# A two-layer hybrid decoder trunk in split fp32: eight PSUM buffers dealt out as four and four, and the output projection taken by halves of its contraction

## The chip, the cores and the metric

The kernel runs on one core of one Trainium2 chip. The metric is the time of one execution on the device, in microseconds (us). Engines: PE is TensorE (matmuls; PEld is its weight load), DVE is VectorE, ACT is ScalarE, POOL is GpSimd, SP issues the DMAs. PSUM, into which PE writes, has eight banks; each tile of this kernel takes one bank.

## The reference, cut to what matters

Two layers act on a sequence of 256 tokens with 1024 channels. Every layer normalises its input and multiplies it with one wide input weight. From the product three branches are made: retention, a dilated window attention, and a gated depthwise convolution with a layer norm. Each is multiplied by a SiLU gate and projected back to 1024 channels; sigmoid gates merge the three; the output projection closes the layer.

```python
h = rms_norm(x, norm_w)
z = h @ w_in + b_in
rq, rk, rv, rg, aq, ak, av, ag, cu, cg, mg = jnp.split(z, split_points, axis=-1)
...
y_ret = (r * jax.nn.silu(rg)) @ ret_w_o
...
y_att = (a * jax.nn.silu(ag)) @ att_w_o
...
c = jax.nn.silu(layer_norm(c, conv_norm_w, conv_norm_b))
y_conv = (c * jax.nn.silu(cg)) @ conv_w_o
gates = jax.nn.sigmoid(mg).reshape(B, S, N_BRANCHES, D)
merged = gates[:, :, 0] * y_ret + gates[:, :, 1] * y_att + gates[:, :, 2] * y_conv
return x + merged @ w_out
```

After the second layer a last RMS norm makes the output.

## The kernel before

The weights are cut into units of 1024 rows by 256 columns, which `order()` lists; the main loop takes one unit per step. A unit is named by its kind and number: `ya`, `yc` are the projections of attention and convolution (four units each), `mc` the merge gates of the convolution, `wo` the output projection, `cs` and `cl` the two halves of the convolution's input, with which the next layer begins.

Each float32 operand is split into a high and a low part of a type that PE takes faster, and a product is the sum of three matmuls (high by high, high by low, low by high). In step n `load(n + 3)` issues the DMAs of a weight unit into two half tiles `raw`, and `split(n + 2)` makes `whi` on ACT (line 218) and `wlo` on DVE (line 219), a half tile at a time. `raw`, `whi` and `wlo` have five half tiles each. So the second half of unit n + 2 goes where the first half of unit n was, and has to wait until PE has read that for the last time. `split` stands in the program ahead of the matmuls of step n, so on ACT and DVE everything that step n issues afterwards is queued behind it.

There are four ways through a unit. `gemm` and `gemm_values` take the eight slices of k in order, 48 matmuls of 256 columns, and are done with the first half tile at half of the step. `gemm_wide` takes two neighbouring units as a couple, 512 columns at once: a step covers four of the eight slices of k, first for tokens 0 to 127 (t = 0), then for tokens 128 to 255 (t = 1), 24 matmuls, so the first half tile is read again in the second half, until 18 of 24. `gemm_two` does likewise for the first two `wo` units, with 48 matmuls; the other two `wo` units go through `gemm`.

The order on all engines is that of the program. Work is put aside with `later` and played at four places of a step: `after_split`, `inside` (in the middle of the matmuls), `first` (after the matmuls) and `due` (after the unit's own evacuation). What the change touches:

- PSUM tiles come from rings named by tag: `g` (products, 3 buffers), `S` (2), `pt` (2), `u` (1). A new tile of a ring waits until the oldest has been read.
- `branch` (lines 686 and 687) multiplies a finished half of a `yc` couple by its gate and adds it to `m`. `merged` turns four 128 by 128 blocks of `m` on PE (line 699, tile `mt`) and makes from them the operand `mh` of the output projection, its high part on ACT (line 702) and its low part on DVE (line 703).
- `ln_add`, `ln_mean`, `ln_rows` make the mean of the layer norm: DVE adds the channels (`ca`), PE sums over partitions (`ss`, line 330), DVE makes the mean and two diagonal matrices `dg` (line 351), and PE spreads them over the partitions (`rb`, line 357).
- `project` adds a `wo` unit to `x` (line 708); its inner function `rest` squares it (`sq`, line 365) and makes two slices of the next layer's operand `gx`, high part on ACT (line 377), low part on DVE (line 378). The first three `cs` and `cl` steps of the next layer read `gx`, slice after slice.
- `project_last` does it for the last layer, with the transposes `nat` (`turn_out`, line 727) and the sums of squares that end the kernel.

Of the kernel before, what the change touches and what calls it, by code (L numbers as in the profile page):

```python
# [142 lines left out]
def trunk(ctx: ExitStack, tc, xp, wp, b_in, params, consts, out):  # L143
# [42 lines left out]
    def load(n, parts=((0, 4), (4, 8))):  # L186
        if n >= N:
            return
        raw_t[n] = ts = [sb.tile([128, 4, W], F32, tag="raw", name="raw", bufs=5) for _ in range(2)]
        if n in couple:  # L190
            n0 = couple[n]
            src = wp[n0:n0 + 2].rearrange("u p (k n) -> p k u n", n=W)
            for q in range(2):
                k = 4 * (n - n0) + 2 * q
# [26 lines left out]

    def gemm(n, a):

        hs, ls = hi_t.pop(n), lo_t.pop(n)
        k_first = n + 1 < N
        if k_first:
            t = ps.tile([128, 2, W], F32, tag="g", name="g", bufs=3)
            p = halves(t)
        else:
            t = p = [ps.tile([128, W], F32, tag="g", name=f"g{j}", bufs=3) for j in range(2)]  # L230

        def part(j, k):
            wh, wl = hs[k // 4][:, k % 4, :], ls[k // 4][:, k % 4, :]
            t = slice(j * 128, j * 128 + 128)
            trio = ((wh[:, t], a[:, k, 0, :]), (wh[:, t], a[:, k, 1, :]), (wl[:, t], a[:, k, 0, :]))
            for i, (u, v) in enumerate(trio):
                PE.matmul(p[j], u, v, start=(k == 0 and i == 0 and (j == 0 or not k_first)),  # L237
                          stop=(k == NK - 1 and i == 2 and (j == 1 or not k_first)))

        if k_first:  # L240
            for k in range(NK):
                if k == 4:
                    play(inside, n)
                for j in range(2):
                    part(j, k)
        else:
            for j in range(2):
                if j == 1:
                    play(inside, n)
                for k in range(NK):  # L250
                    part(j, k)
        return t

    def gemm_values(n, a):

        hs, ls = hi_t.pop(n), lo_t.pop(n)
        t = ps.tile([128, 2, W], F32, tag="g", name="g", bufs=3)
        for k in range(NK):
            if k == 4:
                play(inside, n)  # L260
            wh, wl = hs[k // 4][:, k % 4, :], ls[k // 4][:, k % 4, :]
            for j in range(2):
                r = slice(j * 128, j * 128 + 128)
                for i, (u, v) in enumerate(((0, wh), (0, wl), (1, wh))):
                    PE.matmul(t[:, j], a[:, k, u, r], v, start=(k == 0 and i == 0 and j == 0),  # L265
                              stop=(k == NK - 1 and i == 2 and j == 1))
        return t

    def gemm_wide(n, a, between):

        hs, ls = hi_t.pop(n), lo_t.pop(n)
        half = n - couple[n]
        if half == 0:
            st["wide"] = [ps.tile([128, 2, W], F32, tag="g", name="g", bufs=3) for _ in range(2)]
        for t, p in enumerate(st["wide"]):
# [10 lines left out]
        return st["wide"][1]  # L286

    def gemm_two(n, a):

        hs, ls = hi_t.pop(n), lo_t.pop(n)  # L290
        half = n - couple[n]
        if half == 0:
            st["two"] = [ps.tile([128, 2, W], F32, tag="g", name="g", bufs=3) for _ in range(2)]
        for u, p in enumerate(st["two"]):
            if u == 1:
                play(inside, n)
            for c in range(4):
                k, d = 4 * half + c, 2 * (c % 2) + u
                wh, wl = hs[c // 2][:, d, :], ls[c // 2][:, d, :]
                for j in range(2):  # L300
                    t = slice(j * 128, j * 128 + 128)
                    trio = ((wh[:, t], a[:, k, 0, :]), (wh[:, t], a[:, k, 1, :]), (wl[:, t], a[:, k, 0, :]))
                    for i, (w, v) in enumerate(trio):
                        PE.matmul(p[:, j], w, v, start=(k == 0 and i == 0 and j == 0),  # L304
                                  stop=(k == NK - 1 and i == 2 and j == 1))
        return st["two"]
# [16 lines left out]
    def token_sums(tiles, ss=None, more=False):  # L323

        start = ss is None
        if start:
            ss = ps.tile([128, 2], F32, tag="S", name="ss")
# [26 lines left out]
    def spread(dg):  # L354
        p = ps.tile([128, S], F32, tag="u", name="rb", bufs=1)
# [173 lines left out]
    def ret_scores(l, h):  # L529
        q, k = st.pop((l, "q", h)), st.pop((l, "k", h))  # L530
        s = ps.tile([128, 384], F32, tag="S", name="rs")
# [10 lines left out]
    def ret_out(l, h):  # L542
        sm, v = st.pop((l, "rsm", h)), st[l, "rv", h - h % 2][:, :, h % 2]
        r = ps.tile([128, 2, W], F32, tag="u", name="r", bufs=1)
# [12 lines left out]
    def ret_back(l, h):  # L557
# [4 lines left out]
        p = ps.tile([128, 2, S], F32, tag="pt", name="rt")  # L562
# [19 lines left out]
    def att_scores(l, pair, g):  # L582
# [6 lines left out]
        for j in range(2):  # L589
            s = ps.tile([128, 2, 128 if g else 256], F32, tag="S", name="as")  # L590
# [29 lines left out]
    def att_turn(l, pair, j, part):  # L620
# [3 lines left out]
        p = ps.tile([128, 2, S], F32, tag="pt", name="pt")  # L624
# [8 lines left out]
    def att_pv(l, pair, j):  # L633
        pts = [st.pop((l, "pts", j, part)) for part in range(2)]
        u = ps.tile([128, S], F32, tag="u", name="u", bufs=1)
# [41 lines left out]
    def branch(l, i, b, n, t, p):  # L677
# [10 lines left out]
        if b == 2:  # L688
            if t == 0:
                later(n, merged, l, i, t, at=first)  # L690
            else:
                later(n + 1, merged, l, i, t, at=inside)

    def merged(l, i, t):

        m, mh = st[l, "m"], st[l, "mh"]
        p = ps.tile([128, 4, 128], F32, tag="pt", name="mt")
# [7 lines left out]
    def project(l, i, n, p):  # L705
# [8 lines left out]
        if i < 3:  # L714
# [5 lines left out]
    def turn_out(k):  # L720
        if k == 0:
            st["nat"] = {}
        for t in range(2):
            half = k // 4
            if k % 4 == 0:
                st["nat"][t, half] = ps.tile([128, 512], F32, name="nat", **NAT[t, half])
            PE.transpose(st["nat"][t, half][:, (k % 4) * 128:(k % 4) * 128 + 128],
                         st["xf"][:, k, t * 128:t * 128 + 128], ident)

    NAT = {(0, 0): dict(tag="pt"), (1, 0): dict(tag="pt"), (0, 1): dict(tag="S"), (1, 1): dict(tag="u", bufs=1)}  # L730
# [4 lines left out]
    def project_last(l, i, n, p):  # L735
        if i == 0:
            st["xf"] = sb.tile([128, NK, S], F32, tag="cacc", name="xf", bufs=1)
        sqs = []
        for j in range(2):
            k = 2 * i + j  # L740
            DVE.tensor_tensor(x[:, k], p[j], x[:, k], ALU.add)
            if i < 3:
                later(n + 1, turn_out, k, at=inside if i == 2 else due)
            else:
                sq = sb.tile([128, S], F32, tag="pts1", name="sq")
                ACT.activation(sq, x[:, k], AF.Square)
                sqs.append(sq)
            DVE.tensor_scalar(st["xf"][:, k], x[:, k], prm[:, P_FINAL + k:P_FINAL + k + 1], None, ALU.mult)
        if i < 3:
            add_squares((l + 1, "sq"), x[:, 2 * i:2 * i + 2], i == 0, i == 2)  # L750
            if i == 2:
                later(n + 1, early_sums, l + 1, at=inside)
            return
        r = rstd(token_sums(sqs, st["ss"]), NORM_EPS)
        turn_out(6)
        turn_out(7)
        for half in range(2):
            for t in range(2):
                o = sb.tile([128, 512], F32, tag="gt", name="o", bufs=4)
                if t == 0:  # L760
                    ACT.mul(o, st["nat"][t, half], r[:, t:t + 1])
                else:
                    DVE.tensor_scalar(o, st["nat"][t, half], r[:, t:t + 1], None, ALU.mult)
# [3 lines left out]
    def finish(n, p):  # L767
        l, kind, i = units[couple.get(n, n)]
# [12 lines left out]
        else:  # L781
            for q, pq in enumerate(p if n in couple else [p]):
                if l + 1 < DEPTH:
                    project(l, i + q, n, pq)
                else:
                    project_last(l, i + q, n, pq if n + 1 == N else halves(pq))

    def finish_wide(n, t, p):
        l, kind, i = units[couple[n]]
        if kind in ("rv", "av"):  # L790
            wide_values(l, kind, i, t, p)
        elif kind in ("mr", "ma", "mc"):
            merge_gate(l, i, kind, t, p)
        else:
            branch(l, i, ("r", "a", "c").index(kind[1]), n, t, p)
# [8 lines left out]
    for l in range(DEPTH):  # L804
# [23 lines left out]
        later(y + 2, ln_mean, l)  # L828
# [23 lines left out]
    def warm_up():  # L852
# [3 lines left out]
        p = ps.tile([128, S], F32, tag="u", name="warm", bufs=1)  # L856
# [7 lines left out]
    with tc.manual_schedule():  # L864
# [24 lines left out]
        for n, (l, kind, i) in enumerate(units):  # L889
# [24 lines left out]
            if kind == "wo" and n in couple:  # L914
                p = gemm_two(n, src)
            elif n in couple:
                p = gemm_wide(n, src, lambda t, p: finish_wide(n, t, p))
# [10 lines left out]
            if n in couple and kind != "wo":  # L928
                if n > couple[n]:
                    finish_wide(n, 1, p)  # L930
            elif n not in couple or n > couple[n]:
                finish(n, p)
            play(due, n)
# [51 lines left out]
```

## Time and profile before

| what | value |
|---|---|
| median of three runs | 1234.7 us (1229.91 to 1234.83) |
| the profiled execution: time / span | 1232.1 us / 1230.3 us |
| PE, PEld busy | 1202.2 us (98%), 1117.9 us (91%) |
| DVE, ACT busy | 976.9 us (79%), 750.3 us (61%) |
| PE's waits for other engines, all | 21.7 us |
| mean granted clock of PE | 0.994 |
| DMA | 214.61 MB, 174 GB/s |

The span runs from the first to the last instruction; 1.8 us of the execution lie around it. Matmuls overlap, so a busy share of 98% isn't an engine at its peak: how long a stretch of matmuls takes is read from their starts.

### The profile page before, as it was taken

The numbers are of one execution on the slowest core, as the hardware profiler recorded it, in microseconds if no ns is written. First come the engines' busy times: TensorE is split into PE (matmuls) and PEld (weight loads), VectorE is DVE, ScalarE is ACT, GpSimd is POOL, SyncE is SP. The second block draws the span as 40 slices with busy tenths as digits, with TensorE's granted clock in tenths as the row PEclk, the third lists the DMA queues.
The fourth block names the chain that finished last, engine by engine and source line by source line (L and its number), as shares of the span: only waits on it lengthen the run. The fifth ranks groups of instructions, "written<-read, shape, count | busy, mean of one in ns | idle before, by whom it ended". The sixth has DMA issues, their size and how long they took to land.

```text
span 1230.3 us, 21469 instructions
## 1 busy us (share of the span) xinstructions
PE 1202.2 (98%) x8260; PEld 1117.9 (91%) x8260; DVE 976.9 (79%) x1705; ACT 750.3 (61%) x1116; POOL 9.2 (1%) x17
## 2 busy tenths in 40 slices
PE   9999999999999999999899999999999999999987
PEld 8999989999999989787899989799999999987977
DVE  6978798888888877775689788989787878768654
ACT  6535467877677666464455446586868686754732
POOL 0000000000000000000000000000000000000000
PEclk9999999999999999999999999999999999999999
DMA  8754566555545565555445554655554545565640
GB/s 310 232 181 145 156 209 196 160 178 166 165 158 179 159 196 182 173 194 169 158 153 186 166 189 140 219 172 181 168 176 146 184 153 169 180 197 179 193 126 35
DMA packets 126711, 214.61 MB, mean 174 GB/s; under 512 B 9744, under 2 KB 95504, under 8 KB 126480
## 3 DMA queue, kind: packets, MB, share of 16 engines
q1 hardware_dynamic: 126608, 213.24, 54.4%
q8 instruction: 65, 1.06, 0.3%
q14 instruction: 38, 0.31, 0.1%
HBM read 212.15 MB, written 1.05 MB: 173 GB/s over the span
## 4 chain that ended last, share of the span: by engine, by line
PE 80%; issue 8%; DVE 6%; DMA 2%; ACT 2%; SPq 0%; POOL 0%; DVEq 0%; POOLq 0%; ACTq 0%
PE g L237 45%; PE g L285 23%; PE g L265 4%; DVE wlo L219 3%; PE as L594 2%; DMA raw<-in_wp 2%; PE u L646 1%; PE pt L628 1%; ACT whi L218 1%; PE g L304 1%; DVE cacc L437 1%; PE rs L533 1%; PE u L641 1%; DMA bb<-in_b_in 0%; ACT Sm L609 0%
## 5 line engine op out<-in xcount | busy, mean ns | idle before, releaser
L219 DVE TENSOR_TENSOR wlo<-raw,whi 128x1024 fp32r<-128x1024 f32 (+1 forms) x387 | 456.0, 1212 | 113.0 <-ACT whi L218 108.5
L218 ACT CAST whi<-raw 128x1024 fp32r<-128x1024 f32 (+1 forms) x387 | 391.7, 1043 | 200.1 <-PE g L285 112.6
L237 PE MATMUL g<-h,whi 128*128 128x256 f32 x1664 | 300.8, 283 | 0.0
L237 PEld LDWEIGHTS g<-h,whi 128*128 128x128 f32 x1664 | 257.3, 189 | 0.8
L237 PE MATMUL g<-h,wlo 128*128 128x256 f32 x832 | 235.1, 283 | 0.0
L237 PE MATMUL g<-hp,whi 128*128 128x256 f32 x1280 | 233.9, 285 | 0.0
L437 DVE SCALAR_TENSOR_TENSOR cacc<-cpad,prm,cacc 128x256 f32<-128x256 f32 x480 | 201.4, 478 | 0.5 <-ACT cacc L434 0.4
L237 PEld LDWEIGHTS g<-hp,whi 128*128 128x128 f32 x1280 | 200.3, 192 | 0.9
L237 PE MATMUL g<-hp,wlo 128*128 128x256 f32 x640 | 181.0, 283 | 0.0
L285 PE MATMUL g<-whi,h 128*128 128x512 f32 x512 | 166.2, 398 | 1.3 <-DVE vw L526 1.3
L237 PEld LDWEIGHTS g<-h,wlo 128*128 128x128 f32 x832 | 156.7, 188 | 0.0
L285 PE MATMUL g<-whi,gated 128*128 128x512 f32 x384 | 122.6, 395 | 2.7 <-DVE mg L673 2.7
L237 PEld LDWEIGHTS g<-hp,wlo 128*128 128x128 f32 x640 | 122.7, 192 | 0.0
L285 PEld LDWEIGHTS g<-whi,h 128*128 128x128 f32 x512 | 96.4, 188 | 23.9 <-DVE vw L526 2.2
L285 PE MATMUL g<-wlo,h 128*128 128x512 f32 x256 | 101.0, 394 | 0.0
L285 PEld LDWEIGHTS g<-whi,gated 128*128 128x128 f32 x384 | 73.0, 190 | 18.7 <-DVE mg L673 3.6
L285 PE MATMUL g<-whi,hp 128*128 128x512 f32 x256 | 82.3, 393 | 0.0
L285 PE MATMUL g<-wlo,gated 128*128 128x512 f32 x192 | 75.5, 393 | 0.0
L504 DVE TENSOR_TENSOR zz<-zz,cst 128x512 f32<-128x512 f32 x48 | 33.2, 692 | 52.0 <-ACT zz L503 52.0
L237 PE MATMUL g<-gx,whi 128*128 128x256 f32 x384 | 72.4, 291 | 1.5 <-ACT whi L218 1.5
L501 ACT ACTIVATE z<-g,prm 128x256 f32<-128x256 f32 x96 | 45.7, 476 | 31.1 <-PE g L237 11.2
L237 PEld LDWEIGHTS g<-gx,whi 128*128 128x128 f32 x384 | 62.0, 198 | 1.9 <-ACT whi L218 1.7
(155 smaller groups left out, 1529.2 us busy)
## 6 DMA issues: line engine op xcount, KB each, us to landing
raw<-in_wp SPq DMA_DIRECT2D x230, 512.0 KB, 4.9
raw<-in_wp SPq DMA_DIRECT2D x307, 256.0 KB, 4.2
bb<-in_b_in SPq DMA_DIRECT2D x56, 128.0 KB, 4.5
cst<-in_consts SPq DMA_DIRECT2D x1, 1408.0 KB, 8.1
out_y<-o SPq DMA_DIRECT2D x4, 256.0 KB, 2.4
xt<-in_xp SPq DMA_DIRECT2D x3, 256.0 KB, 5.4
cst<-in_consts SPq DMA_DIRECT2D x1, 384.0 KB, 5.8
prm<-in_params SPq DMA_DIRECT2D x1, 360.0 KB, 5.3
```

The source lines that it names most:

```text
L218: ACT.copy(h, t)
L219: DVE.tensor_tensor(lo, t, h.bitcast(F32), ALU.subtract)
L237: PE.matmul(p[j], u, v, start=(k == 0 and i == 0 and (j == 0 or not k_first)), stop=(k == NK - 1 and i == 2 and (j == 1 or not k_first)))
L265: PE.matmul(t[:, j], a[:, k, u, r], v, start=(k == 0 and i == 0 and j == 0), stop=(k == NK - 1 and i == 2 and j == 1))
L285: PE.matmul(p, a[:, k, u, r], v, start=(k == 0 and i == 0), stop=(k == NK - 1 and i == 2))
L304: PE.matmul(p[:, j], w, v, start=(k == 0 and i == 0 and j == 0), stop=(k == NK - 1 and i == 2 and j == 1))
L437: DVE.scalar_tensor_tensor(c[:, 2 * i + j], cp[:, j, t:t + S], col(l, P_TAP + (2 * i + j) * TAPS + t), c[:, 2 * i + j], ALU.mult, ALU.add)
L501: ACT.activation(z[:, j], p[:, j], AF.Identity, bias=b)
L504: DVE.tensor_tensor(zz, zz, two(cst[:, sin:sin + S]), ALU.mult)
L533: PE.matmul(s[:, 0:256], k[:, d, 0:128], q[:, d, :], start=(d == 0), stop=(d == 1))
L594: PE.matmul(s[:, r], q[:, j, t], k[:, j, t] if g else k[:, j, :], start=True, stop=True)
L628: PE.transpose(p[:, i, r * 128:r * 128 + 128], sm[:, r, o:o + 128], ident)
```

## The change

The rings become two: `g` with four buffers, and `S` with four for every other PSUM tile. The four `wo` units go through `gemm_two` as two couples, in the order: k 0 to 3 of the first couple, k 0 to 3 of the second, k 4 to 7 of the first, k 4 to 7 of the second; their DMAs take the form of the coupled units. `merged` for t = 0 is played in the middle of the next step, and for t = 1 after its matmuls; before it was right after the step, and in the middle of the next one. In a coupled step the first result is handed on (`done`) ahead of what is played `inside`. `ln_mean` moves from the end of the third `ya` step into the middle of the fourth. `project`'s `rest` is put aside for the first two units only. In the last unit the two column halves are finished one after the other in separate banks, over k 4 to 7 alone.

```diff
 def couples(units):
...
-        if kind in WIDE and i % 2 == 0 or kind == "av" and 4 <= i < 8 or kind == "wo" and i == 0:
-            c[n] = c[n + 1] = n
+        if kind in WIDE and i % 2 == 0 or kind == "av" and 4 <= i < 8:
+            c[n], c[n + 1] = (n, 0), (n, 1)
+        elif kind == "wo":
+            c[n] = (n - i + 2 * (i % 2), i // 2)
...
+    def bank():
+        return ps.tile([128, 2, W], F32, tag="g", name="g", bufs=4)
...
-    def gemm_wide(n, a, between):
+    def gemm_wide(n, a, done):
...
             if t == 1:
                 play(inside, n)
-                if half:
-                    between(0, st["wide"][0])
...
+            if half and t == 0:
+                done(0, p)
...
-    def gemm_two(n, a):
+    def gemm_two(n, a, done):
...
+            whole = bank(), bank()
+            st["two", n0] = [halves(t) for t in whole], whole
+            if n0 + 2 == N:
+                st["two", n0][0][1][1] = ps.tile([128, W], F32, tag="S", name="g", bufs=4)
...
+            last = n0 + u + 1 == N
+            for j, c in ((j, c) for j in range(2) for c in range(4)) if last else ((j, c) for c in range(4) for j in range(2)):
...
+            if half and u == 0:
+                done(0, whole[0])
...
     def spread(dg):
-        p = ps.tile([128, S], F32, tag="u", name="rb", bufs=1)
+        p = ps.tile([128, S], F32, tag="S", name="rb", bufs=4)
...
         if b == 2:
-            if t == 0:
-                later(n, merged, l, i, t, at=first)
-            else:
-                later(n + 1, merged, l, i, t, at=inside)
+            later(n + 1, merged, l, i, t, at=first if t else inside)
...
-        if i < 3:
+        if i < 2:
             later(n + 1, rest, at=after_split)
         else:
             rest()
...
-    def project_last(l, i, n, p):
+    def project_last(l, i, p):
+
         if i == 0:
             st["xf"] = sb.tile([128, NK, S], F32, tag="cacc", name="xf", bufs=1)
+        k = 2 * i
+        if i < 3:
+            DVE.tensor_tensor(x[:, k:k + 2], p, x[:, k:k + 2], ALU.add)
+            add_squares((l + 1, "sq"), x[:, k:k + 2], i == 0, i == 2)
...
+            if i < 2:
+                later(N - 1, turn_out, k + j, at=inside)
         if i < 3:
-            add_squares((l + 1, "sq"), x[:, 2 * i:2 * i + 2], i == 0, i == 2)
-            if i == 2:
-                later(n + 1, early_sums, l + 1, at=inside)
             return
+        early_sums(l + 1)
+        turn_out(4)
+        turn_out(5)
...
-        later(y + 2, ln_mean, l)
+        later(y + 3, ln_mean, l, at=inside)
```

Three places show what stands where. First PE, from the end of the second `yc` step of layer 0 to the middle of the third (`mt` is the turned block, `g<-whi,gated` a matmul of `yc`). Before:

```order
L285 MATMUL g<-wlo,gated 128x512
L285 MATMUL g<-whi,gated 128x512
L699 MATMUL mt<-cst,m 128x128 x4
L285 MATMUL g<-whi,gated 128x512
L285 MATMUL g<-wlo,gated 128x512
```

Now, at the same place and up to the next `mt`:

```order
L275 MATMUL g<-whi,gated 128x512 x2
L275 MATMUL g<-wlo,gated 128x512
L275 MATMUL g<-whi,gated 128x512 x2
L275 MATMUL g<-wlo,gated 128x512
L275 MATMUL g<-whi,gated 128x512 x2
L275 MATMUL g<-wlo,gated 128x512
L275 MATMUL g<-whi,gated 128x512 x2
L275 MATMUL g<-wlo,gated 128x512
L275 MATMUL g<-whi,gated 128x512
L692 MATMUL mt<-cst,m 128x128 x4
L275 MATMUL g<-whi,gated 128x512
```

The four transposes of t = 0 have moved from the seam of two steps to behind the first twelve matmuls of the next step.

Second DVE, in the third and fourth `ya` step of layer 0 (`wlo` is `split`, `mean` and `dg` belong to `ln_mean`, `mg` and `m` to `branch`, `rb` is what PE spreads). Before:

```order
L335 TENSOR_TENSOR ca<-ca 128x256
L219 TENSOR_TENSOR wlo<-raw,whi 128x1024 x2
L452 TENSOR_SCALAR mean<-ss 128x2
L351 TENSOR_SCALAR dg<-cst,mean 128x128 x2
L219 TENSOR_TENSOR wlo<-raw,whi 128x1024 x2
L686 TENSOR_TENSOR mg<-g,mg 128x512
L687 TENSOR_TENSOR m<-m,mg 128x512
L686 TENSOR_TENSOR mg<-g,mg 128x512
L687 TENSOR_TENSOR m<-m,mg 128x512
L461 TENSOR_TENSOR cacc<-cacc,rb 128x512 x2
```

Now:

```order
L331 TENSOR_TENSOR ca<-ca 128x256
L222 TENSOR_TENSOR wlo<-raw,whi 128x1024 x4
L682 TENSOR_TENSOR mg<-g,mg 128x512
L683 TENSOR_TENSOR m<-m,mg 128x512
L448 TENSOR_SCALAR mean<-ss 128x2
L347 TENSOR_SCALAR dg<-cst,mean 128x128 x2
L682 TENSOR_TENSOR mg<-g,mg 128x512
L683 TENSOR_TENSOR m<-m,mg 128x512
L457 TENSOR_TENSOR cacc<-cacc,rb 128x512 x2
```

`mean` and `dg` have moved behind the fourth step's two `wlo` and behind the first `mg` and `m`. On PE the matmuls of `rb` still stand right after the fourth step's matmuls.

Third ACT, from the last `whi` of the output projection of layer 0 to the `rows` of layer 1 (`acc` and `sq` are the squares, `gx` the high parts). Before:

```order
L218 CAST whi<-raw 128x1024 x4
L365 ACTIVATE acc<-xt 128x512
L377 ACTIVATE gx<-xt,prm 128x256 x2
L365 ACTIVATE sq<-xt 128x512
L377 ACTIVATE gx<-xt,prm 128x256 x2
L218 CAST whi<-raw 128x1024 x2
L365 ACTIVATE sq<-xt 128x512
L377 ACTIVATE gx<-xt,prm 128x256 x2
L365 ACTIVATE sq<-xt 128x512
L377 ACTIVATE gx<-xt,prm 128x256 x2
```

Now:

```order
L221 CAST whi<-raw 128x1024 x6
L361 ACTIVATE acc<-xt 128x512
L373 ACTIVATE gx<-xt,prm 128x256 x2
L361 ACTIVATE sq<-xt 128x512
L373 ACTIVATE gx<-xt,prm 128x256 x2
L361 ACTIVATE sq<-xt 128x512
L373 ACTIVATE gx<-xt,prm 128x256 x2
L361 ACTIVATE sq<-xt 128x512
L373 ACTIVATE gx<-xt,prm 128x256 x2
```

The two `whi` that stood between the second and the third pair of slices, those of the first `cl` unit of layer 1, now stand ahead of all four. DVE has the same change with `wlo`.

## Rows read from the trace of the kernel before

**Rows 1.** The page: the span, and the busy time of each engine.

```profile
span 1230.3 us, 21469 instructions
...
PE 1202.2 (98%) x8260; PEld 1117.9 (91%) x8260; DVE 976.9 (79%) x1705; ACT 750.3 (61%) x1116; POOL 9.2 (1%) x17
```

**Rows 2.** What PE waited for: line, releaser, us in total, times, longest us.

```profile
PE mt L699 <- DVE m L687: 9.8, 4, 2.5
PE g L285 <- DVE mg L673: 2.7, 2, 1.5
PE g L304 <- DVE mh L703: 2.0, 2, 1.0
...
PE ss L330 <- DVE ca L335: 1.4, 2, 0.7
PE g L285 <- DVE vw L526: 1.3, 2, 1.1
...
PE ss L330 <- DVE acc L335: 1.0, 2, 0.5
```

**Rows 3.** The timeline at the end of the second `yc` step of layer 0, rows of ACT, DVE and PE: start us, duration us, engine, line, what, count, in brackets the idle time before and its releaser.

```profile
568.93 1.05 ACT L218 CAST whi<-raw 128x1024 fp32r<-128x1024 f32 x1 [3.07 <-PE g L285]
...
570.01 1.22 DVE L219 TENSOR_TENSOR wlo<-raw,whi 128x1024 fp32r<-128x1024 f32 x1 [2.90 <-ACT whi L218]
571.16 0.68 DVE L686 TENSOR_TENSOR mg<-g,mg 128x512 f32<-128x512 f32 x1
571.88 0.69 DVE L687 TENSOR_TENSOR m<-m,mg 128x512 f32<-128x512 f32 x1
...
569.82 0.39 PE L285 MATMUL g<-whi,gated 128*128 128x512 f32 x1
572.62 0.66 PE L699 MATMUL mt<-cst,m 128*128 128x128 f32 x4 [2.42 <-DVE m L687]
```

**Rows 4.** Busy times by stretch: the stretch, its length, PE, PEld, DVE, ACT and POOL busy with counts, PE's granted clock, DMA share, GB/s. The first follows the wait of rows 3, the second the next wait for `m` in layer 0, the third the second such wait in layer 1.

```profile
573.40:576.70 3.30, 3.30 (x9) 2.60 (x8) 2.73 (x4) 1.45 (x2) 0.00 (x0) 0.50 0.18 62
...
590.50:593.90 3.40, 3.40 (x30) 3.25 (x29) 2.64 (x4) 0.44 (x1) 0.00 (x0) 1.00 0.00 0
...
1194.60:1198.00 3.40, 3.40 (x19) 3.40 (x17) 3.07 (x4) 0.87 (x1) 0.00 (x0) 0.50 0.00 0
```

**Rows 5.** Pieces of the chain of waits in layer 0, start us and us: undisturbed matmuls of a coupled step, of three steps of 48 matmuls (the last two of the output projection and the first of layer 1), and the first 18 of the fourth `ya` step.

```profile
506.17 4.25 PE g L285 x18
...
559.28 9.59 PE g L285 x42
...
602.96 17.14 PE g L237 x144
```

**Rows 6.** The timeline of the layer norm's mean in layer 0, from the third to after the fourth `ya` step, rows of ACT, DVE and PE.

```profile
510.44 1.06 ACT L218 CAST whi<-raw 128x1024 fp32r<-128x1024 f32 x1 [4.48 <-PE g L285]
...
507.89 0.48 DVE L351 TENSOR_SCALAR dg<-cst,mean 128x128 f32<-128x128 f32 x2
...
511.53 1.23 DVE L219 TENSOR_TENSOR wlo<-raw,whi 128x1024 fp32r<-128x1024 f32 x1 [2.02 <-ACT whi L218]
512.67 0.68 DVE L686 TENSOR_TENSOR mg<-g,mg 128x512 f32<-128x512 f32 x1
513.39 0.69 DVE L687 TENSOR_TENSOR m<-m,mg 128x512 f32<-128x512 f32 x1
514.00 0.68 DVE L686 TENSOR_TENSOR mg<-g,mg 128x512 f32<-128x512 f32 x1
...
511.61 0.61 PE L357 MATMUL rb<-dg,cst 128*128 128x128 f32 x4
```

**Rows 7.** The timeline of the passage from layer 0 to layer 1, rows of ACT and DVE.

```profile
605.73 1.05 ACT L218 CAST whi<-raw 128x1024 fp32r<-128x1024 f32 x1 [1.80 <-PE g L237]
...
607.21 0.90 ACT L377 ACTIVATE gx<-xt,prm 128x256 fp32r<-128x256 f32 x2
...
616.40 0.90 ACT L377 ACTIVATE gx<-xt,prm 128x256 fp32r<-128x256 f32 x2
...
607.95 0.87 DVE L378 SCALAR_TENSOR_TENSOR gx<-xt,prm,gx 128x256 fp32r<-128x256 f32 x2
...
609.34 0.87 DVE L378 SCALAR_TENSOR_TENSOR gx<-xt,prm,gx 128x256 fp32r<-128x256 f32 x2
610.14 0.68 DVE L708 TENSOR_TENSOR xt<-g,xt 128x512 f32<-128x512 f32 x1
...
615.09 0.68 DVE L708 TENSOR_TENSOR xt<-g,xt 128x512 f32<-128x512 f32 x1
616.53 0.69 DVE L367 TENSOR_TENSOR acc<-acc,sq 128x512 f32<-128x512 f32 x1 [0.76 <-ACT sq L365]
...
617.60 0.87 DVE L378 SCALAR_TENSOR_TENSOR gx<-xt,prm,gx 128x256 fp32r<-128x256 f32 x2
...
621.44 0.48 DVE L351 TENSOR_SCALAR dg<-cst,r 128x128 f32<-128x128 f32 x2 [0.80 <-POOL r L345]
```

**Rows 8.** The timeline of PE at the end: the transposes and sums between the two halves of the last unit, and the sum after it.

```profile
1218.12 0.60 PE L727 MATMUL nat<-cst,xf 128*128 128x128 f32 x4
1218.56 0.50 PE L330 MATMUL ss<-cst,acc 128*128 128x1 f32 x4
...
1222.99 0.61 PE L330 MATMUL ss<-cst,sq 128*128 128x1 f32 x4 [0.63 <-ACT sq L746]
```

More of the change, by code (lines that the diff above doesn't have):

```diff
@@ L220, in split, with trio_of @@
         hi_t[n], lo_t[n] = hs, ls
+    def bank():
+        return ps.tile([128, 2, W], F32, tag="g", name="g", bufs=4)
+    def trio_of(a, k, wh, wl):
+        return (wh, a[:, k, 0, :]), (wh, a[:, k, 1, :]), (wl, a[:, k, 0, :])
     def gemm(n, a):
         hs, ls = hi_t.pop(n), lo_t.pop(n)
[L225 to L228, printed above, removed]
-        else:
[L230 to L246, printed above, removed]
-            for j in range(2):
[L248 to L252, printed above, removed]
+        p = bank()
+        for k in range(NK):
+            if k == 4:
+                play(inside, n)
+            for j in range(2):
+                t = slice(j * 128, j * 128 + 128)
+                for i, (w, v) in enumerate(trio_of(a, k, hs[k // 4][:, k % 4, t], ls[k // 4][:, k % 4, t])):
+                    PE.matmul(p[:, j], w, v, start=(k == 0 and i == 0 and j == 0),
+                              stop=(k == NK - 1 and i == 2 and j == 1))
+        return p
     def gemm_values(n, a):
         hs, ls = hi_t.pop(n), lo_t.pop(n)
-        t = ps.tile([128, 2, W], F32, tag="g", name="g", bufs=3)
+        p = bank()
         for k in range(NK):
@@ L264, in gemm_values @@
                 for i, (u, v) in enumerate(((0, wh), (0, wl), (1, wh))):
-                    PE.matmul(t[:, j], a[:, k, u, r], v, start=(k == 0 and i == 0 and j == 0),
+                    PE.matmul(p[:, j], a[:, k, u, r], v, start=(k == 0 and i == 0 and j == 0),
                               stop=(k == NK - 1 and i == 2 and j == 1))
-        return t
-    def gemm_wide(n, a, between):
+        return p
+    def gemm_wide(n, a, done):
         hs, ls = hi_t.pop(n), lo_t.pop(n)
-        half = n - couple[n]
+        n0, half = couple[n]
         if half == 0:
-            st["wide"] = [ps.tile([128, 2, W], F32, tag="g", name="g", bufs=3) for _ in range(2)]
-        for t, p in enumerate(st["wide"]):
+            st["wide"] = [bank(), bank()]
+        for t in range(2):
+            p = st["wide"][t]
             if t == 1:
                 play(inside, n)
-                if half:
-                    between(0, st["wide"][0])
             r = slice(t * 128, t * 128 + 128)
@@ L285, in gemm_wide @@
                     PE.matmul(p, a[:, k, u, r], v, start=(k == 0 and i == 0), stop=(k == NK - 1 and i == 2))
-        return st["wide"][1]
-    def gemm_two(n, a):
+            if half and t == 0:
+                done(0, p)
+        return p
+    def gemm_two(n, a, done):
         hs, ls = hi_t.pop(n), lo_t.pop(n)
-        half = n - couple[n]
+        n0, half = couple[n]
         if half == 0:
-            st["two"] = [ps.tile([128, 2, W], F32, tag="g", name="g", bufs=3) for _ in range(2)]
-        for u, p in enumerate(st["two"]):
+            whole = bank(), bank()
+            st["two", n0] = [halves(t) for t in whole], whole
+            if n0 + 2 == N:
+                st["two", n0][0][1][1] = ps.tile([128, W], F32, tag="S", name="g", bufs=4)
+        parts, whole = st["two", n0]
+        for u in range(2):
             if u == 1:
                 play(inside, n)
[L297 to L306, printed above, removed]
+            last = n0 + u + 1 == N
+            for j, c in ((j, c) for j in range(2) for c in range(4)) if last else ((j, c) for c in range(4) for j in range(2)):
+                k, d, t = 4 * half + c, 2 * (c % 2) + u, slice(j * 128, j * 128 + 128)
+                for i, (w, v) in enumerate(trio_of(a, k, hs[c // 2][:, d, t], ls[c // 2][:, d, t])):
+                    PE.matmul(parts[u][j], w, v, start=(k == 0 and i == 0 and (j == 0 or last)),
+                              stop=(k == NK - 1 and i == 2 and (j == 1 or last)))
+            if half and u == 0:
+                done(0, whole[0])
+        return parts[1] if last else whole[1]
     def hi_lo(dst, k, v, nk, n=None):
@@ L721, in turn_out @@
         if k == 0:
-            st["nat"] = {}
+            st["nat"] = [[ps.tile([128, 512], F32, tag="S", name="nat", bufs=4) for _ in range(2)]]
+        if k == 4:
+            st["nat"].append([bank().rearrange("p a b -> p (a b)") for _ in range(2)])
         for t in range(2):
[L724 to L727, printed above, removed]
+            PE.transpose(st["nat"][k // 4][t][:, (k % 4) * 128:(k % 4) * 128 + 128],
@@ L738, in project_last @@
         sqs = []
         for j in range(2):
[L740 to L744, printed above, removed]
+            if i == 3:
+                DVE.tensor_tensor(x[:, k + j], p[j], x[:, k + j], ALU.add)
                 sq = sb.tile([128, S], F32, tag="pts1", name="sq")
-                ACT.activation(sq, x[:, k], AF.Square)
+                ACT.activation(sq, x[:, k + j], AF.Square)
@@ L760, in project_last @@
                 if t == 0:
-                    ACT.mul(o, st["nat"][t, half], r[:, t:t + 1])
+                    ACT.mul(o, st["nat"][half][t], r[:, t:t + 1])
                 else:
-                    DVE.tensor_scalar(o, st["nat"][t, half], r[:, t:t + 1], None, ALU.mult)
+                    DVE.tensor_scalar(o, st["nat"][half][t], r[:, t:t + 1], None, ALU.mult)
                 SP.dma_start(out[t * 128:t * 128 + 128, half * 512:half * 512 + 512], o)
     def finish(n, p):
-        l, kind, i = units[couple.get(n, n)]
+        l, kind, i = units[n]
         if kind == "cs":
@@ L780, in finish, with finish_half @@
             gated(l, i, COLS[kind][1], "c" if kind == "cg" else "ru", n, p)
[L781 to L789, printed above, removed]
+    def finish_half(n, t, p):
+        l, kind, i = units[couple[n][0]]
         if kind in ("rv", "av"):
@@ L913, in trunk @@
                 src = st[l, "g" if kind in ("cs", "cl") and i < UNSCALED else "h"]
[L914 to L917, printed above, removed]
+            if n in couple:
+                p = (gemm_two if kind == "wo" else gemm_wide)(n, src, lambda t, p: finish_half(n, t, p))
             elif kind == "av":
@@ L927, in trunk @@
                 continue
[L928 to L931, printed above, removed]
+            if n not in couple:
                 finish(n, p)
+            elif couple[n][1]:
+                finish_half(n, 1, p)
             play(due, n)
```

32 lines of the change are left out of this document (17 added, 15 removed).

## The prediction, made before the result was known

> **What bounds the kernel now.** I read the page first: of a span of 1230.3 us PE is busy for 98% [rows 1]. So only what PE loses can be won, and the second view is the list of what PE waited for [rows 2]. It is short, and nearly all of it stands in three places of each layer: before the transposes of the merged branches (9.8 us in four waits) and in the output projection behind them (2.0), where a coupled step wants a bank that is still being read (2.7 and 1.3), and at the sums of the layer norm (1.4 and 1.0). These are 18.2 us in 14 waits. A wait costs a little more than its row says, since the next matmuls start from an empty pipeline: in [rows 3] the last matmul starts at 569.82, the transposes at 572.62, and at the pace of 9.59 / 42 = 0.228 us [rows 5] they would have started at 570.05: 2.57 lost, where the wait is put at 2.42. I add 0.15 us for each of the 14, 2.1 in all: 20.3 us.
>
> Third, the stretches behind the waits. After the first wait for `m` in layer 0 and the second in layer 1 the granted clock is 0.50, which is 1.2 GHz, for 3.3 to 3.4 us; after the other in layer 0 it is 1.00, which is 2.4 GHz [rows 4]. In a stretch at half the clock PE does half the work, so each costs 1.7 us: 3.4 us.
>
> Fourth, the timeline shows why PE waits for `m` [rows 3]. ACT's cast of a weight half waits until PE has read the old half, at 18 of the 24 matmuls of the coupled step; then come `wlo`, `mg` and `m` on DVE, in this order, and `m` is ready at 572.57, 2.5 us after the end of the matmuls. This pattern, a step's DVE work coming out 2.5 us after the step because it is queued behind `wlo`, is what the change has to get round, and it decides below where it runs into it anew.
>
> **The change part by part.** All durations are of the profiled execution, whose time is 1232.1 us: its span and 1.8 us around it; the median of the three runs shown is 2.6 us higher.
>
> *Merged branches half a step later.* The transposes for t = 0 now stand behind 12 more matmuls, 12 x 0.228 = 2.73 us after the end of the step; `m` is there after 2.5 us [rows 3], so there are 0.2 us to spare. At the seam to `wo` it is 24 x 0.119 = 2.86 us (17.14 / 144 is 0.119 us a matmul) [rows 5]. Those for t = 1 stand a whole step behind it. All four waits go: 9.8 + 0.6.
>
> *The output projection by halves of k.* The matmuls stay 48 a step, so PE's work is the same. k 4 to 7 are wanted only in the third `wo` step, a step after `mh` is made: the waits for `mh` go, 2.0 + 0.3. With these waits both stretches at half the clock go, 3.4. Together 16.1 us.
>
> *Four banks for products.* A couple takes two new banks while the couple before it still holds two; with four there is no fourth wait to inherit. The rows whose releaser is the reader of a bank (`mg`, `vw`) go [rows 2]: 2.7 + 1.3 + 0.6 = 4.6 us. The Trainium skill (Perfetto Trace Analysis, Optimization Strategy) says that the same gap repeating on the engine that should be saturated can mean too little SBUF or PSUM for the next tile. Here that rule covers these four waits alone; were it the cause of all 14, the change would win all of them, which is a rival below.
>
> *Four banks for everything else.* Nothing in [rows 2] waits for a tile of the old rings `S`, `pt` and `u`, though `u` had one buffer. In attention twelve tiles are made per pair, and the fourth-last is always of an earlier step. I take 0; the bound above is a rival below, the bound below is 0, since there is no wait to remove.
>
> *`ln_mean` in the middle of the fourth `ya` step.* The wait for `ca` goes: 1.4 + 0.3. But now `dg` is late. It stands on DVE behind the fourth step's `wlo`, `mg` and `m`, and the matmuls of `rb` follow that step's matmuls at once. In [rows 5, 6]: 18 matmuls are read by 510.42, the cast starts at 510.44, `wlo` at 511.53, `mg` at 512.67, `m` at 513.39, and the place behind `m` is 514.00. There `mean` and `dg` would start; `dg` would follow `mean` as before, 0.2 us behind, and take 0.48: ready at 514.68. PE was ready for `rb` at 511.61. So PE waits 3.1 us, once in each layer: 6.2 us. Behind PE's `rb` stands the whole `mc` stage. The waits before were 2.4 us, and two of four were followed by a stretch at half the clock; these are longer, so I take 1.7 us after each, 3.4 (between 0 and 3.4). In return DVE catches up while PE waits: it applies `rb` right behind it, where before it came after a second `mg` and `m` (514.00 and 1.3 more, 3.7 us behind 511.61), and the wait for `acc` at the next sum goes: 1.0 + 0.3. The layer norm as a whole: -3.0 + 6.2 + 3.4 = 6.6 us lost.
>
> *The passage to layer 1.* Before, the first two `rest` had been worked off a step before layer 1 began; now all four stand behind the cast of the last weight half, which waits for matmul 36 of the 48 of the last `wo` step (a `gemm_two` reads its first half tile again; the `gemm` that stood there let it go at 24). Let E be the end of that step. The cast starts at E - 12 x 0.119 = E - 1.4. With the distances of [rows 7] from the cast at 605.73: the high parts of slices 0 and 1 start 1.5 later, the low parts of 0 and 1 are done at E + 1.3 and E + 1.7, of 2 and 3 at E + 2.65 and E + 3.1; then DVE adds the third unit to `x` at 4.41, that is E + 3.0. From such an add (615.09) to the low parts it is 1.3 us to the high parts (616.40), 2.1 to the end of `acc` (617.22), 0.43 for each low part: slices 4 and 5 at E + 5.55 and E + 6.0. The fourth add follows at E + 5.9, and with the fold of the sums its low parts take until 2.9 and 3.4 after it [rows 7]: E + 8.85 and E + 9.3. PE wants slice k at E + 0.71 k, six matmuls each, and the low part for the second of them. It waits some 1.1 us for slice 0, 1.4 for slice 4, 1.9 for slice 6, and ends the step at about E + 10.2 where 48 x 0.119 = 5.7 would do: 4.5 us lost, once. Before, slice 7 was ready at 618.47, and that step ended at 602.96 + 17.14 = 620.10 [rows 5, 7], so it was wanted at 619.4: hidden, with 0.9 us to spare. Below, the loss is 0 if the order let the slices out earlier; above it is 4.5 + 1.7 with a stretch at half the clock. I take 4.5, as the waits are short and broken by matmuls.
>
> *The end.* Four transposes and four sums between the halves of the last unit, 1218.12 to 1218.92 or 0.8 us [rows 8], go behind the last matmul, where PE waited 0.6 us for the squares anyway. DVE's chain for the third unit now starts half a step before the end and puts the last add back by some 0.25 us. I take 0.5 us won (between 0.8 won and 0.5 lost).
>
> *DMAs.* The last two `wo` units of each layer come in four DMAs instead of two, same bytes; PE waits for no DMA in [rows 2], and the casts are held by PE, not by landing, in [rows 3, 6, 7]. 0.
>
> The sum: won 16.1 + 4.6 + 0.5 = 21.2; lost 6.6 + 4.5 = 11.1; net 10.1 us won. 1232.1 - 10.1 = 1222.0, and 1224.6 from the median. I predict 1223 us. With no stretch at half the clock after `rb` it is 13.5 won, 1218.6; with one more in the passage 8.4 won, 1223.7 or 1226.3 from the median. About 0.5% (6.2 us) is what a measurement of this kernel can tell from no change.
>
> **The rivals.**
>
> *No new wait.* If want of banks, and not DVE's queue, is behind the waits, then `dg` and the slices come in time too, and the change wins 21.2 and the 3.0 of the layer norm: 1232.1 - 24.2 = 1208 us. For it: DVE has 21% idle. Against it: the idle time lies ahead of `wlo`, in waiting for the cast [rows 6], and `m` is named as the releaser, not a bank's reader [rows 2]. The Trainium skill's rule on repeating gaps, named above, would come out here.
>
> *The gain is given back.* The passage leaves ACT and DVE behind at the start of layer 1, whose first steps carry `zr`, `hf` and the taps, so the weights of the second `cs` step come late too. Price: another wait like that for slices 4 and 6, 1.4 + 1.9, and 1.7 of clock, 5.0 us: 10.1 - 5.0 = 5.1 won, 1227 to 1229.6. It speaks for it that slice 7 now ends some 0.9 us before the end of the step instead of 1.6. Against it: DVE is seen to wait 0.8 us for POOL soon after [rows 7], and so has time to catch up.
>
> *Slower.* One ring for scores, transposes and outputs makes PE wait in attention: if a score tile finds the fourth-last tile unread, PE waits as it did for a bank, 1.35 us (2.7 over 2) [rows 2]. Two such waits in each of the eight pairs are 21.6 us: 1222 + 21.6 = 1243.6. It decides from 8 waits on (10.8 us), which undo the gain. For it: DVE is busy for 79%, and its taps stand between the scores of a pair. Against it: before, a score tile waited for the second-last one and PE never waited there.
>
> **How the numbers follow.** The forecast, both new waits and a net gain of 8.4 to 13.5 us: 0.64. No new wait: 0.11. Given back: 0.17. Slower: 0.08, of which 0.02 end within 0.5%. So faster 0.64 + 0.11 = 0.75, and of the second rival's 0.17 a tenth is beyond the bound: 0.76; within 0.5% 0.18; slower 0.06. The forecast alone spans 1218 to 1226; to leave out no more than 2 in 10 I reach to 1214 and to 1231.
>
> **What would show it.** In the profile after: no wait for `m` before `mt`, none for `mh`, none for `mg` or `vw` at a bank; a wait of `rb` for `dg` of some 3 us twice; waits of `g<-gx` for the low parts in one step of layer 1 adding to 4.5 us. If `rb` does not wait, I have misread the queue on DVE; if the passage costs nothing, the largest single term of the loss is wrong; a new row for `as`, `pt` or `u` would be the rival that is slower.

## The result, and the profile after

The changed kernel takes 1219.53 us (median of four runs, 1217.52 to 1221.11) against 1233.98 us before: a ratio of 0.9888, with a 95% interval of 0.9862 to 0.9915. That is 14.4 us faster. Forecast were 1223 us, with 1214 to 1231 as the range. The profiled execution took 1217.5 us, 14.6 less than that of before.

The page after, where [rows 1] show it before:

```profile
span 1215.5 us, 21472 instructions
...
PE 1197.6 (99%) x8260; PEld 1116.8 (92%) x8260; DVE 976.2 (80%) x1702; ACT 751.1 (62%) x1116; POOL 9.2 (1%) x17
```

DVE and ACT do the same work as before. Of the 14.8 us that the span lost, 10.2 are time in which PE stood still; PE's busy time fell by 4.6. All that PE still waited for (compare [rows 2]; line, releaser, us in total, times, longest):

```profile
PE rb L353 <- DVE dg L347: 5.7, 2, 2.8
PE g L241 <- ACT gx L373: 1.5, 3, 0.5
PE g L241 <- DVE gx L374: 1.5, 3, 0.8
PE g L241 <- ACT whi L221: 1.4, 1, 1.4
PE warm L851 <- DVE zero L848: 1.2, 1, 1.2
PE g L241 <- DVE wlo L222: 0.2, 1, 0.2
```

Not one of the six rows that [rows 2] show is left: no wait for `m`, `mh`, a bank's reader, `ca` or `acc`. The last three rows are the start of the kernel and were there before. The first three are new, 8.7 us in all, and stand where the prediction put them.

That the transposes of t = 0 now find `m` ready, if only just, is seen behind the second `yc` step of layer 0 (compare [rows 3]):

```profile
572.34 0.69 DVE L683 TENSOR_TENSOR m<-m,mg 128x512 f32<-128x512 f32 x1
...
573.23 0.60 PE L692 MATMUL mt<-cst,m 128*128 128x128 f32 x4
```

`m` is done at 573.03, 0.2 us before PE reaches the transposes.

The first of the new waits is at the layer norm's mean. DVE and PE in the fourth `ya` step of layer 0 (compare [rows 6]):

```profile
508.20 1.23 DVE L222 TENSOR_TENSOR wlo<-raw,whi 128x1024 fp32r<-128x1024 f32 x1 [1.64 <-ACT whi L221]
509.34 0.68 DVE L682 TENSOR_TENSOR mg<-g,mg 128x512 f32<-128x512 f32 x1
510.06 0.69 DVE L683 TENSOR_TENSOR m<-m,mg 128x512 f32<-128x512 f32 x1
510.67 0.15 DVE L448 TENSOR_SCALAR mean<-ss 128x2 f32<-128x2 f32 x1
510.85 0.48 DVE L347 TENSOR_SCALAR dg<-cst,mean 128x128 f32<-128x128 f32 x2
```
```profile
508.07 0.39 PE L275 MATMUL g<-whi,gated 128*128 128x512 f32 x1
511.29 1.19 PE L353 MATMUL rb<-dg,cst 128*128 128x128 f32 x4 [2.83 <-DVE dg L347]
```

`wlo`, `mg` and `m` run ahead of `mean` and `dg`, and PE goes from its last matmul at 508.07 to `rb` at 511.29, where 0.23 us would do: 3.0 us lost, in each layer. The stretches right behind it (columns as in [rows 4]), first of layer 0, then of layer 1:

```profile
511.30:514.50 3.20, 3.20 (x10) 2.72 (x11) 2.52 (x5) 1.21 (x3) 0.00 (x0) 0.50 0.63 237
1112.90:1116.30 3.40, 3.40 (x17) 2.88 (x18) 2.67 (x5) 1.49 (x3) 0.00 (x0) 1.00 0.70 231
```

At half the clock the matmuls of 512 columns start 0.43 us apart, at the full clock 0.23. It happened in layer 0 and not in layer 1.

The second is the passage to layer 1, the PE rows with a wait:

```profile
606.74 0.38 PE L241 MATMUL g<-gx,whi 128*128 128x256 f32 x1 [0.54 <-ACT gx L373]
607.47 0.39 PE L241 MATMUL g<-gx,whi 128*128 128x256 f32 x1 [0.35 <-DVE gx L374]
610.92 0.38 PE L241 MATMUL g<-gx,whi 128*128 128x256 f32 x1 [0.44 <-ACT gx L373]
611.64 0.38 PE L241 MATMUL g<-gx,whi 128*128 128x256 f32 x1 [0.34 <-DVE gx L374]
613.76 0.38 PE L241 MATMUL g<-gx,whi 128*128 128x256 f32 x1 [0.55 <-ACT gx L373]
614.95 0.39 PE L241 MATMUL g<-gx,whi 128*128 128x256 f32 x1 [0.80 <-DVE gx L374]
```

The pairs are slices 0, 4 and 6: first the high part from ACT is missing, then the low part from DVE. What DVE did in between shows the chain (compare [rows 7]):

```profile
605.79 1.23 DVE L222 TENSOR_TENSOR wlo<-raw,whi 128x1024 fp32r<-128x1024 f32 x1 [2.15 <-ACT whi L221]
606.93 0.88 DVE L374 SCALAR_TENSOR_TENSOR gx<-xt,prm,gx 128x256 fp32r<-128x256 f32 x2
...
609.11 0.69 DVE L701 TENSOR_TENSOR xt<-g,xt 128x512 f32<-128x512 f32 x1
```

DVE stood idle for 2.15 us ahead of this `wlo`, with the slices queued behind it.

The rows of waits don't tell what a wait costs in all. For that, take the same matmul in both kernels and compare its start in the two profiles (us; both have 8260 matmuls):

| PE's matmul | start before | start now | ahead by |
|---|---|---|---|
| last one that stood ahead of the first wait for a bank, layer 0 | 172.63 | 172.32 | 0.3 |
| last one that stood ahead of the sum of `ca`, layer 0 | 504.49 | 502.12 | 2.4 |
| last of the second `yc` step, layer 0 | 569.82 | 570.28 | -0.5 |
| last of the output projection, layer 0 | 614.07 | 605.92 | 8.2 |
| last of the first step of layer 1 | 619.82 | 616.23 | 3.6 |
| last one that stood ahead of the sum of `ca`, layer 1 | 1110.41 | 1103.64 | 6.8 |
| last of the second `yc` step, layer 1 | 1175.75 | 1170.28 | 5.5 |
| last of the last but one `wo` step, layer 1 | 1214.27 | 1200.23 | 14.0 |
| end of the span | 1230.3 | 1215.5 | 14.8 |

From line to line: 0.3 us are won at the start, 2.1 by the banks in layer 0, 2.8 are lost around the layer norm, 8.6 are won by the transposes and the projection, and 4.6 are lost in the passage; then, in layer 1, 3.2 are won by the banks, 1.3 lost around the layer norm, 8.6 won by the transposes and the projection, and 0.8 at the end.

### The profile page after: what moved, and what is told of

Its sections match the earlier page's. It is cut to its first block, busy times and chain, and to the rows that moved or that the text cites. A ratio compares the mean times of both kernels' runs of the same rounds, so it can differ in the third digit from the quotient of the medians.

```text
span 1215.5 us, 21472 instructions
## 1 busy us (share of the span) xinstructions
PE 1197.6 (99%) x8260; PEld 1116.8 (92%) x8260; DVE 976.2 (80%) x1702; ACT 751.1 (62%) x1116; POOL 9.2 (1%) x17
## 4 chain that ended last, share of the span: by engine, by line
PE 90%; issue 7%; DVE 1%; ACT 1%; DMA 1%; SPq 0%; POOLq 0%; POOL 0%; DVEq 0%; ACTq 0%
PE g L241 47%; PE g L275 29%; PE g L256 4%; PE as L590 2%; PE g L298 2%; PE u L642 1%; PE pt L624 1%; PE rs L529 1%; PE u L637 1%; DVE wlo L222 0%; ACT whi L221 0%; DMA xt<-in_xp 0%; PE rs L531 0%; PE u L638 0%; PE rt L561 0%
```

## The experiments

The theory under test: what PE waits for in this kernel is late because of its place in an in-order queue, behind a weight split (`whi` on ACT, `wlo` on DVE) that itself waits until PE has read the old weights. The rivals: too few PSUM banks, or too much work on DVE and ACT in these places, so that a wait taken away here comes back there. In all of them the output is computed in full. The ratios are to the kernel before, run on the same chip.

**e1. The changed kernel with the mean back where it was.**

```diff
-        later(y + 3, ln_mean, l, at=inside)
+        later(y + 2, ln_mean, l)
```

> The changed kernel with ln_mean back at the end of the third ya step. Queue theory (dg is late only because it stands on DVE behind the fourth step's wlo, mg and m): the two waits of rb (3.0 us each from start to start) and the half-clock stretch behind one of them (1.7) go, the waits for ca (0.85 each) and acc (0.65 each) come back: 7.7 won, 3.0 lost, 1215 us (1213 to 1217). Rival (the move is right and rb is late because of DVE's total load): rb waits as long as before, and the waits for ca come on top: 1221 us.

Measured: 1214.21 us (1213.59 to 1214.65), ratio 0.9840 (0.9827 to 0.9854). `rb` no longer waits; the waits for `ca` and `acc` are back, 1.6 and 1.2 us. The queue theory holds: this part of the change by itself costs some 5 us (1219.53 against 1214.21).

**e2. The last `wo` step's weight split behind the slices.**

```diff
-            if not late:
+            if not late and (kind, i) != ("wo", 3):
                 split(n + 2)
...
             play(due, n)
+            if (kind, i) == ("wo", 3):
+                split(n + 2)
```

> The changed kernel with the weight split of the last wo step of each layer put at the end of that step, behind the four adds and the slices of gx. Queue theory (the slices are late because they stand behind a cast that waits for PE): slices 0 to 3 are ready before layer 1 begins, the waits for gx (4.3 us from start to start in the changed kernel) fall to 0.5 or less, no new wait: 1215.5 us (1214.5 to 1217). Rival (ACT and DVE have too much work there, whatever the order): the waits move to the weights of the first cl step, g<-gx for whi or wlo, some 3 to 4 us, 1219 us.

Measured: 1216.43 us (1214.70 to 1217.23), ratio 0.9857 (0.9843 to 0.9870). The waits in layer 1 and at `rb`:

```profile
PE rb L353 <- DVE dg L347: 5.7, 2, 2.8
...
PE g L241 <- DVE gx L374: 0.5, 1, 0.5
PE g L241 <- DVE wlo L222: 0.5, 2, 0.3
```

Of 3.0 us for `gx` 0.5 are left, and no wait for weights came in its place: both waits for `wlo` lie in the first 15 us of the kernel. So ACT and DVE were not overloaded in the passage; they worked in the wrong order. By the starts of the same matmuls the passage takes 3.8 us less than in the changed kernel. The gain in the medians is 3.1 us, a little under the 4.0 expected. In this profile both waits of `rb` were followed by slow stretches, in layer 0 by two in a row; the third row is of layer 1:

```profile
510.20:513.50 3.30, 2.59 (x8) 2.33 (x9) 3.21 (x8) 0.58 (x1) 0.00 (x0) 0.50 0.93 314
513.60:516.90 3.30, 3.30 (x9) 2.61 (x8) 1.92 (x2) 1.48 (x2) 0.00 (x0) 0.50 0.04 16
1111.00:1114.40 3.40, 3.40 (x10) 2.63 (x9) 2.46 (x5) 2.16 (x3) 0.00 (x0) 0.51 0.33 121
```

**e3. The fourth `ya` step's weight split behind `mg`, `m`, `mean` and `dg`.**

```diff
-            late = n < 3 or (kind, i) == ("cs", 0)
+            late = n < 3 or (kind, i) in (("cs", 0), ("ya", 3))
```

> The changed kernel with the weight split of the fourth ya step put behind that step's first mg, m, mean and dg. Queue theory: dg is ready 2.3 us after the middle of the step, 0.4 us before its end, so rb does not wait and no half-clock stretch follows: 7.7 won; the wait for acc may come back with up to 1.3: 1212.5 us (1211 to 1215). Rival (DVE's total load): the work only changes places, and mc's weights or the sums wait 2 to 3 us in each layer instead: 1218 us.

Measured: 1210.30 us (1209.83 to 1210.63), ratio 0.9809 (0.9795 to 0.9822). There is no row for `rb`, none for `ca`, none for `acc`. The expected price, a wait for `acc` of up to 1.3 us, did not come. The time is 0.7 us below the range that was expected: 7.7 us were to be won on the changed kernel, and the medians lie 9.2 apart, the two profiled executions 7.3. The runs of the changed kernel have mean clocks of 0.993 to 0.995, those of e3 0.997 to 0.999.

**e4. Both late splits.**

> Both late splits together, the fourth ya step's and the last wo step's. Queue theory: the two gains add, 7.7 + 3.8 less up to 1.3: 1208.5 us (1207 to 1212). Rival (total load of ACT and DVE): 1217 us or more.

Measured: 1207.24 us (1206.04 to 1207.57), ratio 0.9783 (0.9770 to 0.9796): faster than both kernels, and 26.7 us faster than the one before (1233.89 in these runs). All waits of PE:

```profile
PE g L241 <- ACT whi L221: 1.6, 1, 1.6
PE warm L851 <- DVE zero L848: 1.2, 1, 1.2
PE g L241 <- DVE gx L374: 0.5, 1, 0.5
PE g L241 <- DVE wlo L222: 0.2, 1, 0.2
```

DVE in the fourth `ya` step, with PE's `rb` after it:

```profile
505.77 0.68 DVE L682 TENSOR_TENSOR mg<-g,mg 128x512 f32<-128x512 f32 x1
506.49 0.69 DVE L683 TENSOR_TENSOR m<-m,mg 128x512 f32<-128x512 f32 x1
507.10 0.15 DVE L448 TENSOR_SCALAR mean<-ss 128x2 f32<-128x2 f32 x1
507.29 0.48 DVE L347 TENSOR_SCALAR dg<-cst,mean 128x128 f32<-128x128 f32 x2
507.69 2.35 DVE L222 TENSOR_TENSOR wlo<-raw,whi 128x1024 fp32r<-128x1024 f32 x2
```
```profile
508.74 0.61 PE L353 MATMUL rb<-dg,cst 128*128 128x128 f32 x4
```

The same instructions, in another order: `dg` is done a microsecond before PE wants it, and the two `wlo` are still done at 510.04, some 4 us before the step that needs them.

**e5. The kernel before with only the rings changed** (four buffers for `g`, one ring of four for all else; two of the last transposes take their banks from `g`).

```diff
-            t = ps.tile([128, 2, W], F32, tag="g", name="g", bufs=3)
+            t = ps.tile([128, 2, W], F32, tag="g", name="g", bufs=4)
...
-        p = ps.tile([128, S], F32, tag="u", name="rb", bufs=1)
+        p = ps.tile([128, S], F32, tag="S", name="rb", bufs=4)
...
-    NAT = {(0, 0): dict(tag="pt"), (1, 0): dict(tag="pt"), (0, 1): dict(tag="S"), (1, 1): dict(tag="u", bufs=1)}
+    NAT = {(0, 0): dict(tag="S", bufs=4), (1, 0): dict(tag="S", bufs=4), (0, 1): dict(tag="g", bufs=4), (1, 1): dict(tag="g", bufs=4)}
```

> The kernel before with only the rings changed: four banks for products, four shared by all other tiles. Queue theory: only the four waits for a bank's reader (mg and vw, 4.7 us from start to start) go, the waits for m stay: 1229.2 us (1228 to 1231). Rival (want of banks is behind all the waits): the waits for m, mh, ca and acc go too, 1210 to 1214 us. Rival (a ring of four shared by scores, transposes and outputs makes PE wait in attention): new rows for as, pt or u, 1240 us or more.

Measured: 1228.57 us (1226.40 to 1230.78), ratio 0.9961 (0.9946 to 0.9976), 4.9 us less than 1233.44.

```profile
PE mt L699 <- DVE m L687: 9.9, 4, 2.5
PE g L304 <- DVE mh L703: 2.0, 2, 1.0
...
PE ss L330 <- DVE ca L335: 1.6, 2, 0.8
...
PE ss L330 <- DVE acc L335: 1.2, 2, 0.6
```

The waits for a bank's reader, 4 of the 14, are gone, and all others stay within 0.2 us of what they were. There is no row for `as`, `pt` or `u`: the rival by which the shared ring makes the kernel slower has fallen. The Trainium skill's rule on repeating gaps (Perfetto Trace Analysis, Optimization Strategy) covers these 4 waits here and not the other 10.

**e6. The kernel before with only the later transposes.**

```diff
-            if t == 0:
-                later(n, merged, l, i, t, at=first)
-            else:
-                later(n + 1, merged, l, i, t, at=inside)
+            later(n + 1, merged, l, i, t, at=first if t else inside)
```

> The kernel before with only the transposes of the merged branches half a step later. Queue theory: the four waits for m go (10.4 us) and the half-clock stretches with them (3.4); but k 4 to 7 are still wanted in the second wo step, right behind the transposes of t = 1, so the wait for mh grows from 1.3 to between 1.6 and 2.5 us a layer: 1221.5 us (1219 to 1224). Rival (the projection by halves of k is what wins): the wait for m only moves into the second wo step, 4 to 5 us a layer, 1229 us.

Measured: 1218.09 us (1218.01 to 1218.55), ratio 0.9878 (0.9861 to 0.9896): as fast as the whole change, and 0.9 us below the range that was expected. The waits for `m` are gone, and the mean granted clock is 0.999. What it leaves behind is `mh`; the first row is of the start of the kernel:

```profile
PE g L237 <- ACT whi L218: 2.6, 1, 2.6
...
PE g L304 <- ACT mh L699: 1.4, 2, 0.7
...
PE g L304 <- DVE mh L700: 1.1, 2, 0.6
```

These are 2.5 us where there were 2.0, or 1.25 a layer, less than the 1.6 to 2.5 that were expected. This is what the projection by halves of k takes away; in the changed kernel the passage, with its new order, gives 4.6 us back for it. The projection by halves was not run without the rest, since two open couples need four banks, so its own share is not shown.

**e7. The kernel before with the split put back in the second and fourth `yc` step, and nothing else.**

```diff
-            if not late:
+            held_back = kind == "yc" and i % 2 == 1
+            if not late and not held_back:
                 split(n + 2)
...
             play(due, n)
+            if held_back:
+                split(n + 2)
```

> The kernel before with one edit of its own: in the second and fourth yc step the weight split is put at the end of the step, behind mg and m; rings, transposes and projection as before. Queue theory (m is late only because it stands behind wlo, which waits for PE): m for t = 0 is ready 1.1 us before the end of the step, the waits for m fall from 10.4 us to under 1 and the half-clock stretches go; the wait for mh stays at 1.3 to 2 us a layer: 1220.5 us (1219 to 1223), as much as the whole change. Rival (the place of the transposes at the seam is what costs): waits for m of 2 us or more remain, 1230 us.

Measured: 1219.36 us (1218.49 to 1219.53), ratio 0.9886 (0.9871 to 0.9901). PE has no row for `m`, though the transposes stand at the seam as before. DVE:

```profile
567.66 0.69 DVE L686 TENSOR_TENSOR mg<-g,mg 128x512 f32<-128x512 f32 x1 [1.77 <-PE g L285]
568.38 0.69 DVE L687 TENSOR_TENSOR m<-m,mg 128x512 f32<-128x512 f32 x1
```

`mg` now waits for PE alone, not for `wlo` as in [rows 3]. So the place of the transposes was never at fault; the queue ahead of `m` was.

**e8. The changed kernel with the transposes back at the seam.**

```diff
-            later(n + 1, merged, l, i, t, at=first if t else inside)
+            if t == 0:
+                later(n, merged, l, i, t, at=first)
+            else:
+                later(n + 1, merged, l, i, t, at=inside)
```

> The changed kernel with the transposes of the merged branches back at the end of the step and in the middle of the next one. Queue theory: the four waits for m come back (10.4 us), and one to three half-clock stretches more (1.7 each); mh is still not waited for, since k 4 to 7 come in the third wo step: 1232.5 us (1230 to 1236). Rival (banks and the projection by halves have taken the cause away): 1220 us.

Measured: 1234.88 us (1231.49 to 1236.05), ratio 1.0008 (0.9998 to 1.0019): the whole gain is gone.

```profile
PE mt L695 <- DVE m L683: 9.9, 4, 2.5
PE rb L353 <- DVE dg L347: 5.7, 2, 2.8
```

## Why the prediction was right

The direction, the mechanism and the time (1219.5 for 1223, within the range) came out; point by point:

- *Merged branches later, and the projection by halves.* Put at 16.1 us together, with the slow stretches behind the waits; by the starts of the matmuls they won 17.2. All four waits for `m` went, and the 0.2 us to spare were enough; `mh` is not waited for any more. The later transposes alone (e6) bring as much as the whole change, and without them (e8) the gain is gone.
- *Banks.* Put at 4.6 us; 4.9 alone (e5), 5.2 by the starts.
- *The shared ring.* Put at 0; no wait for it in any run.
- *The layer norm.* The wait of `rb` was put at 3.1 us a layer and cost 3.0, and the waits for `ca` and `acc` went, as said. But the loss of 6.6 us was mis-sized: it is 4.1 (2.8 in layer 0, 1.3 in layer 1). I took a stretch at half the clock after each `rb`, 3.4 us in all; the profile has one, and the two layers differ by 1.5. That there was only one is luck: in e2, with the same two waits, the same places lost 2.8 us more.
- *The passage.* Put at 4.5 us, and 4.6 by the starts: from the last matmul of the projection at 605.92 to the last of the next step at 616.23 are 10.3 us, where 48 x 0.119 = 5.7 would do. The waits are at slices 0, 4 and 6, as said. Only half of them is for the low parts, 1.5 us by the rows; as much is for the high parts, which come late behind the same cast. The rows add up to 3.0, so here the row of a wait tells two thirds of its cost.
- *The end.* Put at 0.5 won, and 0.8 by the starts. PE's last weight matmul starts at 1206.80, 8.7 us before the end of the span; before it was 1221.74 and 8.6. So the end costs nothing more, and the 0.8 us of transposes and sums that stood between the halves are won almost whole.

The forecast of 10.1 us won is 4.7 short of the 14.8 by which the span fell. The layer norm gives 2.5 of it, 1.9 of these by the clock; the transposes and the projection 1.1, the banks 0.6, the end 0.3, and the start of the kernel, ahead of all these places, another 0.3. Only the passage was worse than forecast, by 0.1, so the right time does not come from errors that cancel.

## What to carry to other kernels

Where an engine works in program order, ask of each late result what stands ahead of it in its queue, and whether that waits for the very engine that will want the result: here a prefetch of weights, not urgent for a whole step, waited for PE and held up what PE wanted next. Moving the prefetch behind the urgent work cost nothing and won as much in one edit (e7) as the whole change, and on top of the change 12 us more (e4). When a piece of work is moved, look again at what it now stands behind in its queue: the same change that cured one such wait made two new ones.

## What was not expected

The stretch at half the clock does not belong to a place. The same program, with the same wait of 2.8 us before `rb` in both layers, ran on at 2.4 GHz behind one and at 1.2 GHz behind the other; in e2 it followed both, and once for 6.7 us. Before the change two of the four waits of 2.4 to 2.5 us had been followed by one. Nor does it go by the length of the wait. Near the start of the kernel PE waits for a piece of the first weights, 1.4 us in the changed kernel and 2.6 in e6 (the rows for `whi`). These are the stretches behind it, first of the changed kernel, then of e6:

```profile
9.60:12.60 3.00, 3.00 (x16) 3.00 (x16) 2.74 (x6) 2.18 (x6) 0.00 (x0) 0.50 1.02 390
```
```profile
9.40:12.40 3.00, 2.78 (x21) 2.57 (x22) 3.00 (x7) 2.69 (x6) 0.00 (x0) 1.00 1.03 413
```

The shorter wait was followed by half the clock, the longer was not. So such a wait costs PE its own time and, at times, some 1.5 us more, and runs of one kernel differ by it: the four of the changed kernel have mean clocks of 0.993 to 0.995 and lie 3.6 us apart; those of e6, with 0.998 and 0.999, lie 0.5 us apart. What decides whether the clock falls behind a given wait, these runs do not show.
